# One fixed order of the four mixers for the shared preparation buffers in a decoder trunk

## The chip, the cores and the metric

The kernel runs on one core of a Trainium2 chip. The metric is the device time of one execution in microseconds (us), as the median of several runs. A NeuronCore has a matrix engine (TensorE, PE in the profile; its weight loads are the row PEld), a vector engine (VectorE, DVE), a scalar engine (ScalarE, ACT), a general engine (GpSimd, POOL) and a sync engine (SyncE, SP) that issues the DMA transfers here. Each engine works through its own queue strictly in order; they wait for one another by semaphores.

## What is computed

Two layers (DEPTH = 2) of a decoder trunk over 256 tokens of width 1024 in float32. Cut to what matters here:

```python
for l in range(DEPTH):
    h = rms_norm(x, norm1_g[l])
    proj = h @ w_in[l]                      # one projection, split among four mixers and the gates
    ya = dsa_mixer(...)                     # A, sparse: an indexer picks 64 keys per query
    yb = moba_mixer(...)                    # B, block attention
    yc = nsa_mixer(...)                     # C, compressed blocks (an MLP), selected blocks, window
    yd = swa_mixer(...)                     # D, sliding window of 128 with sinks
    br = einsum('bsnc,ncd->bsnd', stack(ya, yb, yc, yd), w_branch[l])
    x = x + (sigmoid(g_br) * br).sum(n) @ w_out[l]
    x = x + conv_ffn(rms_norm(x, norm2_g[l]), w_up[l], conv_w[l], conv_b[l], w_down[l])
```

Every mixer normalises its heads and applies rotary positions before it attends. In C, the raw keys and values are cut into 15 overlapping blocks, and a hidden layer (weights `c_cmp_w1`, then GELU, then `c_cmp_w2`) compresses each.

## The kernel before

**Weights.** All products are made to float32 accuracy from fp32r pieces. A weight chunk is loaded by DMA into one of three buffers `raw`; `split_hi` (ACT) rounds a piece of it to `hi`, `split_lo` (DVE) makes the rest, `lo = raw - hi`; there are four buffers of each. PE multiplies a piece as `hi` with `ahi`, `hi` with `alo` and `lo` with `ahi`, where `ahi` and `alo` are the two parts of the activations. A piece of 128x1024 is 12 matmuls of 512 columns. The stream of these pieces goes through the whole kernel; `SEQ` fixes in which order the merge gates, the hidden layer of C and the branch projections take their chunks: gate 0 (two halves), hidden 0 and 1, gate 1, branch 0, gate 2, branch 1, gate 3 (first half), branch 2, branch 3 (first half), and the last halves.

**Mixers.** Beside this stream run the mixers as generators: `dsa` (A), `moba` (B), `nsa` (C), `swa` (D). Each starts by taking the one set of preparation buffers in the ring `prep_r` (`rt`, `qr`, `kr`, `kn`), forms normalised and rotated queries and keys there on DVE, ACT and POOL (POOL computes the inverse roots `rD`, `rC` and so on by a power), transposes them on PE (`T_pairs`), gives the set back, and spawns its attention (`attend2`: scores, `softmax`, `values`). C prepares more: its rotated keys and copied values are transposed, copied to `kn`, and summed with the block encoding into `kr`, from which `hidden` on PE computes the compression layer with weights that stay in `raw` until it has run. When that sum exists, `hid.ready` is set; `main`, the one generator that emits the weight stream on PE, does not go on past `hidden` before.

**Order.** Nothing of this order is decided on the chip. `Flow.run` is a planner that runs while the kernel is built: again and again it takes, of all generators, the one whose next step can start first by its own clock model, and among equals the one of lower priority number (`PRIO` for the mixers, `urgent` for the pieces, 40 for `main`). The step is emitted at the end of its engine's queue, and there it stays. So the set of preparation buffers goes to whichever mixer's first step the planner sees first. In layer 0 that gave A, B, C, D; in layer 1 it gave A, B, D, C. In this kernel `swa` has priority number 6, in front of `nsa` with 7 and of `moba` with 19.

Where the text speaks of PSUM banks: the weight stream, the scores of the first token half and the hidden layer share the four banks `mm`; the scores of the second half use `sc`; transposes and values use `tr`. All instructions have the helper's line L214 in the profile, so places are found by tile names and by time.

Of the kernel before, what the change touches and what calls it, by code (L numbers as in the profile page):

```python
# [231 lines left out]
def trunk(ctx: ExitStack, tc: tile.TileContext, a, out):  # L232
# [15 lines left out]
    def ring(n, shape, name, dt=F32):  # L248
# [12 lines left out]
    prep_r = Ring([(sb([128, NT, 512], "rt"), sb([128, NT, 256], "qr"), sb([128, NT, 256], "kr"),  # L261
                    sb([128, NT, 256], "kn"))])
# [73 lines left out]
    col_f = [Fut() for _ in range(DEPTH)]  # L336
    tab_f = [Fut() for _ in range(DEPTH)]
# [61 lines left out]
           ("branch", 1, 0), ("branch", 1, 1), ("gate", 3, 0), ("branch", 2, 0), ("branch", 2, 1),  # L399
           ("branch", 3, 0), ("gate", 3, 1), ("branch", 3, 1)]  # L400
    FIRST, LAST = [n for op, n, _ in SEQ if op == "branch"][0], SEQ[-1][1]
    PRIO = (4, 19, 7, 6)
    PORDER = (0, 2, 1, 3)
    CH_A, CH_C = [(0, 384), (384, 680)], [(1448, 1832), (1832, 2100)]
    CH_B, CH_D = [(680, 1192), (1192, 1448)], [(2100, 2612)]
# [393 lines left out]

    def dsa(l, pa, pf, y, yf):  # L800
        m = M[l]
        (prep,) = yield "ACT", [pf, col_f[l]], [prep_r]
        rt, qr, kr, kn = prep
        latT = kn[:, :, 128:256]
        tl = yield from head_rstd(pa[:, :, None, 256:384], 1, 128, sm1["rl"], rt, [])
        tb, = yield "PE", [], [tr_r]
        tp = tb[:, :256].rearrange("p (t q) -> p t q", t=NT)
        for t in range(NT):
            te = P.transpose(tp[:, t, :], pa[:, t, 256:384], ident)
        yield "ACT", [te], []  # L810
        te = A.activation(latT, tp, AF.Copy, scale=m["col"][:, 16:17])
        tr_r.give(tb, te)
        tb, = yield "PE", [te], [tr_r]
        kvp = tb[:, :256].rearrange("p (t q) -> p t q", t=NT)
        for t in range(NT):
            te = P.matmul(kvp[:, t, :], latT[:, t, :], m["kvup"], start=True, stop=True)
        ti = yield from head_rstd(pa[:, :, None, 640:672], 1, 32, sm1["ri"], rt, [])
        yield "DVE", [te, tl], []
        tkv = V.tensor_tensor(kvA, kvp, sm1["rl"][:, :, None].to_broadcast([128, NT, 128]), op=ALU.mult)
        tr_r.give(tb, tkv)  # L820
        yield "DVE", [tab_f[l]], []
        tq = yield from rope(qr.rearrange("p t (h u d) -> p t h u d", u=1, d=32), heads(pa[:, :, 384:640], 32), 8, 32,
                             cosi, sini, rt, [])
        (ix,) = yield "PE", [], [qk_r]
        iqT, ikT = ix[:, 0:512].rearrange("p (k s) -> p k s", k=2), ix[:, 512:768].rearrange("p (k s) -> p k s", k=1)
        tq = yield from T_pairs(iqT, qr, 2, [tq])
        yield "DVE", [ti], []
        ikn = kn[:, :, None, 0:32]
        tn = V.tensor_tensor(ikn, pa[:, :, None, 640:672], sm1["ri"][:, :, None, None].to_broadcast([128, NT, 1, 32]), op=ALU.mult)
        krd = kr[:, :, 0:128]  # L830
        tk = yield from rope(krd.rearrange("p t (h u d) -> p t h u d", h=1, d=32), ikn, 1, 32, ci, si, rt, [tn], dup=4)
        tk = yield from T_pairs(ikT, krd, 1, [tk])
        iw = th(sm1["iw"], 8)
        yield "DVE", [], []
        V.tensor_scalar(iw, pa[:, :, 672:680], 1.0 / 16.0, None, op0=ALU.mult)
        idx_d = []
        idx_f = Fut()
        fin = qk_done(ix, idx_d, idx_f, NT)
        self_f = [Fut() for _ in range(NT)]
        for t in range(NT):  # L840
            fl.spawn(indexer(t, iqT, ikT, iw, [tq, tk], fin, self_f[t]), 5 + t)
        trk = yield from head_rstd(kvA[:, :, None, 0:64], 1, DH, sm1["rk"], rt, [tkv])
        yield "DVE", [trk], []
        knv = kn[:, :, None, 0:64]
        tn = V.tensor_tensor(knv, kvA[:, :, None, 0:64], sm1["rk"][:, :, None, None].to_broadcast([128, NT, 1, 64]), op=ALU.mult)
        tk = yield from rope(krd.rearrange("p t (h u d) -> p t h u d", h=1, d=64), knv, 1, DH, cc[:, 1], ss_[:, 1], rt, [tn], dup=2)
        trq = yield from head_rstd(heads(pa[:, :, 0:256]), H, DH, sm1["rqA"], rt, [])
        yield from scaled(sm1["sA"], sm1["rqA"], H, trq)
        tq = yield from rope(qr.rearrange("p t (h u d) -> p t h u d", u=1, d=64), heads(pa[:, :, 0:256]), H, DH,
                             cc[:, 0], ss_[:, 0], rt, [])  # L850
        (qk,) = yield "PE", [], [qk_r]
        qT, kT = qk[:, 0:512].rearrange("p (k s) -> p k s", k=2), qk[:, 512:768].rearrange("p (k s) -> p k s", k=1)
        tq = yield from T_pairs(qT, qr, 2, [tq])
        tk = yield from T_pairs(kT, krd, 1, [tk])
        prep_r.give(prep, tk)
        fin = qk_done(qk, [], yf, 1)
        fl.spawn(attend2(10, qT, lambda h: 0, kT, lambda h, b: kvA[:, b, 64:128], th(sm1["sA"], H), sel,
                        y, [tq, tk] + self_f, fin=fin), 10)
# [35 lines left out]
        f.t = V.tensor_tensor(sel[t], sel[t], mask, op=ALU.min)  # L894

    def moba(l, pb, pf, y, yf):
        (prep,) = yield "ACT", [pf, tab_f[l]], [prep_r]
        rt, qr, kr, kn = prep
        tr = yield from head_rstd(heads(pb[:, :, 0:512]), 8, DH, sm1["rB"], rt, [])
        yield from scaled(sm1["sB"], sm1["rB"], 8, tr)  # L900
        tq = yield from rope(qr.rearrange("p t (h u d) -> p t h u d", u=1, d=64), heads(pb[:, :, 0:256]), H, DH,
                             cc[:, 2], ss_[:, 2], rt, [])
        (qk,) = yield "PE", [], [qk_r]
        qT, kT = qk[:, 0:512].rearrange("p (k s) -> p k s", k=2), qk[:, 512:1024].rearrange("p (k s) -> p k s", k=2)
        tq = yield from T_pairs(qT, qr, 2, [tq])
        yield "DVE", [], []
        tn = V.tensor_tensor(heads(kn), heads(pb[:, :, 256:512]),
                        th(sm1["rB"], 8)[:, :, 4:8, None].to_broadcast([128, NT, H, DH]), op=ALU.mult)
        tk = yield from rope(kr.rearrange("p t (h u d) -> p t h u d", u=1, d=64), heads(kn), H, DH, cc[:, 3], ss_[:, 3], rt, [tn])
        tk = yield from T_pairs(kT, kr, 2, [tk])  # L910
        prep_r.give(prep, tk)
        fin = qk_done(qk, [], yf, 1)
        fl.spawn(attend2(20, qT, lambda h: h // 2, kT, lambda h, b: pb[:, b, 512 + 64 * h:576 + 64 * h],
                        th(sm1["sB"], H), [tri[:, 128:], tri], y, [tq, tk], fin=fin), 20)

    def swa(l, pd, pf, y, yf):
        (prep,) = yield "ACT", [pf, tab_f[l]], [prep_r]
        rt, qr, kr, kn = prep
        tr = yield from head_rstd(heads(pd[:, :, 0:384]), 6, DH, sm1["rD"], rt, [])
        yield from scaled(sm1["sD"], sm1["rD"], 6, tr)  # L920
        tq = yield from rope(qr.rearrange("p t (h u d) -> p t h u d", u=1, d=64), heads(pd[:, :, 0:256]), H, DH,
                             cc[:, 8], ss_[:, 8], rt, [])
        (qk,) = yield "PE", [], [qk_r]
        qT, kT = qk[:, 0:512].rearrange("p (k s) -> p k s", k=2), qk[:, 512:1024].rearrange("p (k s) -> p k s", k=2)
        tq = yield from T_pairs(qT, qr, 2, [tq])
        yield "DVE", [], []
        knv = heads(kn[:, :, 0:128])
        tn = V.tensor_tensor(knv, heads(pd[:, :, 256:384]),
                        th(sm1["rD"], 6)[:, :, 4:6, None].to_broadcast([128, NT, 2, DH]), op=ALU.mult)
        tk = yield from rope(kr.rearrange("p t (h u d) -> p t h u d", h=2, d=64), knv, 2, DH, cc[:, 9], ss_[:, 9], rt, [tn], dup=2)  # L930
        tk = yield from T_pairs(kT, kr, 2, [tk])
        prep_r.give(prep, tk)
        fin = qk_done(qk, [], yf, 1)
        fl.spawn(attend2(30, qT, lambda h: h // 2, kT,
                        lambda h, b: pd[:, b, 384 + 64 * (h // 2):448 + 64 * (h // 2)], th(sm1["sD"], H),
                        [tri[:, 128:], dmask], y, [tq, tk], sink=M[l]["sink"], fin=fin), 30)

    def nsa(l, pc, pf, y, yf, hid):
        m = M[l]
        (prep,) = yield "DVE", [pf, tab_f[l]], [prep_r]  # L940
        rt, qr, kr, kn = prep
        kvd = kr.rearrange("p t (i u d) -> p t i u d", i=2, u=2)
        t1 = yield from rope(kvd[:, :, 0:1], pc[:, :, None, 256:320], 1, DH, cosd, sind, rt, [], dup=2)
# [322 lines left out]
    def main():  # L1266
# [13 lines left out]
        for l in range(DEPTH):  # L1280
# [11 lines left out]
            proj = (pa, pb, pc, pd)  # L1292
            ys = [p[:, :, 0:256] for p in proj]
            yf = [Fut() for _ in range(4)]
            def mixer(n, f):
                if n == 2:
                    fl.spawn(nsa(l, pc, f, ys[2], yf[2], hid), PRIO[2])
                else:
                    fl.spawn((dsa, moba, None, swa)[n](l, proj[n], f, ys[n], yf[n]), PRIO[n])


            banks = []
            for i, kg in [(0, 0), (1, 0), (0, 1), (1, 1)] + [(i, kg) for i in range(2, len(COLS)) for kg in range(2)]:
                n, c0, c1 = COLS[i]
# [4 lines left out]
                if kg == 1:  # L1309
                    f = Fut()  # L1310
# [176 lines left out]
```

## Time and profile before

| what | before |
|---|---|
| median of 3 runs | 851.69 us (851.65 to 853.23) |
| the profiled execution's own time | 850.18 us |
| its span, first to last instruction | 848.4 us |
| PE matmul busy | 835.4 us, 98% |
| PE weight loads busy | 733.1 us, 86% |
| DVE busy | 673.0 us, 79% |
| ACT busy | 543.8 us, 64% |
| POOL busy | 36.5 us, 4% |
| granted TensorE clock, mean | 0.994 |
| DMA | 149.91 MB, 177 GB/s on average |

The busy shares are averages over stages: the projections, mixers and gates of layer 0 take the time to about 245 us, its feed-forward part that to about 425 us, and layer 1 repeats both. The span leaves out some 1.8 us of the execution's own time, before the first and behind the last instruction.

### The profile page before, as it was taken

To read this page: it belongs to the slowest core of one execution; us is meant where nothing else is said; L and a number is where in the kernel's file an instruction comes from. 1 tells how busy PE (TensorE), PEld (TensorE's weight loads), DVE (VectorE), ACT (ScalarE), POOL (GpSimd) and SP (SyncE) were. 2 spreads that over 40 slices of the span, in tenths; PEclk is the share of its full clock that TensorE was granted. 3 is DMA by queue.
4 is the path that set the end of the run, shared out by engine and by line. 5 is a ranking of instruction groups with operands and counts; after the bars stand their busy time and mean duration, and the time that the engine had idled before them with its cause. 6 is when DMAs were issued, how large, how long until landed. Compare 5 with 4: busy or idle time off the path is not lost.

```text
span 848.4 us, 14190 instructions
## 1 busy us (share of the span) xinstructions
PE 835.4 (98%) x5459; PEld 733.1 (86%) x5459; DVE 673.0 (79%) x1327; ACT 543.8 (64%) x941; POOL 36.5 (4%) x33
## 2 busy tenths in 40 slices
PE   9999999999999999999999997999999999999998
PEld 8987787888899999978898875878878999999886
DVE  5799989788579999975458989977676799999552
ACT  6673775765478888844366667766445788888431
POOL 0111111000000000000001110100000000000000
PEclk9999999999999999999999997999999999999999
DMA  7754563444647666546456453435455465665550
GB/s 264 248 199 149 178 216 106 159 162 153 219 138 229 207 201 197 186 153 210 132 168 211 157 173 115 148 117 182 162 192 192 149 199 199 200 199 199 175 197 26
DMA packets 103414, 149.91 MB, mean 177 GB/s; under 512 B 4072, under 2 KB 62258, under 8 KB 103346
## 3 DMA queue, kind: packets, MB, share of 16 engines
q1 hardware_dynamic: 103346, 149.00, 52.6%
q8 instruction: 43, 0.70, 0.3%
q14 instruction: 25, 0.20, 0.1%
HBM read 147.94 MB, written 1.05 MB: 176 GB/s over the span
## 4 chain that ended last, share of the span: by engine, by line
PE 86%; DVE 7%; DMA 2%; POOL 2%; ACT 1%; issue 1%; SPq 0%; DVEq 0%; ACTq 0%
PE mm L214 75%; PE tr L214 6%; PE sc L214 5%; DVE lo L214 2%; DMA raw<-in_w_in_dram 1%; POOL rB L214 1%; DVE acc L214 1%; DVE rt L214 1%; DMA x<-in_x_dram 1%; POOL rD L214 1%; DVE m L214 1%; DVE f L214 1%; ACT f L214 0%; ACT hi L214 0%; SPq L242 0%
## 5 line engine op out<-in xcount | busy, mean ns | idle before, releaser
L214 DVE TENSOR_TENSOR lo<-raw,hi 128x1024 fp32r<-128x1024 f32 (+2 forms) x280 | 328.7, 1179 | 99.4 <-ACT hi L214 95.3
L214 ACT ACTIVATE hi<-raw 128x1024 fp32r<-128x1024 f32 (+2 forms) x280 | 283.0, 1022 | 152.6 <-PE mm L214 132.4
L214 PE MATMUL mm<-hi,ahi 128*128 128x512 f32 (+4 forms) x480 | 176.0, 372 | 0.6 <-ACT hi L214 0.6
L214 PE MATMUL mm<-hi,alo 128*128 128x512 f32 (+4 forms) x480 | 172.2, 364 | 0.0
L214 PE MATMUL mm<-ahi,hi 128*128 128x256 f32 x640 | 149.9, 276 | 0.0
L214 PE MATMUL mm<-alo,hi 128*128 128x256 f32 x640 | 149.7, 276 | 0.0
L214 PEld LDWEIGHTS mm<-alo,hi 128*128 128x128 f32 x640 | 120.1, 188 | 0.1
L214 PEld LDWEIGHTS mm<-ahi,hi 128*128 128x128 f32 x640 | 120.2, 188 | 0.1
L214 PE MATMUL mm<-lo,ahi 128*128 128x512 f32 (+4 forms) x480 | 118.2, 369 | 0.0
L214 PEld LDWEIGHTS mm<-hi,ahi 128*128 128x128 f32 x480 | 90.2, 188 | 15.2 <-issue 1.7
L214 PEld LDWEIGHTS mm<-hi,alo 128*128 128x128 f32 x480 | 90.3, 188 | 12.0
L214 PEld LDWEIGHTS mm<-lo,ahi 128*128 128x128 f32 x480 | 83.0, 188 | 13.2 <-issue 1.3
L214 PE MATMUL mm<-hi,slotQ 128*128 128x512 f32 x352 | 89.6, 395 | 0.0
L214 PE MATMUL mm<-ahi,lo 128*128 128x256 f32 x640 | 86.9, 276 | 0.0
L214 PEld LDWEIGHTS mm<-hi,slotQ 128*128 128x128 f32 x352 | 66.1, 188 | 15.4
L214 PEld LDWEIGHTS mm<-ahi,lo 128*128 128x128 f32 x640 | 79.1, 188 | 0.0
L214 ACT ACTIVATE f<-f,col 128x256 f32<-128x256 f32 x88 | 48.1, 594 | 6.4 <-DVE f L214 6.4
L214 PE MATMUL mm<-lo,slotQ 128*128 128x512 f32 x176 | 48.7, 396 | 0.0
L214 PEld LDWEIGHTS mm<-lo,slotQ 128*128 128x128 f32 x176 | 33.0, 188 | 7.6
L214 ACT ACTIVATE qk<-f,col 128x256 f32<-128x256 f32 x88 | 39.2, 495 | 0.0
L214 ACT ACTIVATE f<-f,nmx 128x128 f32<-128x128 f32 (+1 forms) x80 | 35.3, 444 | 4.7 <-DVE nmx L214 4.7
L214 DVE SCALAR_TENSOR_TENSOR f<-f,col,f 128x254 f32<-128x254 f32 x88 | 38.2, 478 | 0.0
(235 smaller groups left out, 1038.6 us busy)
## 6 DMA issues: line engine op xcount, KB each, us to landing
raw<-in_w_up_dram SPq DMA_DIRECT2D x44, 1024.0 KB, 5.0
raw<-in_w_in_dram SPq DMA_DIRECT2D x40, 1024.0 KB, 4.8
raw<-in_w_down_dram SPq DMA_DIRECT2D x20, 1024.0 KB, 4.9
raw<-in_w_out_dram SPq DMA_DIRECT2D x8, 1024.0 KB, 5.3
raw<-in_w_branch_dram SPq DMA_DIRECT2D x6, 1024.0 KB
raw<-in_w_in_dram SPq DMA_DIRECT2D x7, 768.0 KB
raw<-in_w_in_dram SPq DMA_DIRECT2D x4, 592.0 KB, 3.7
raw<-in_w_in_dram SPq DMA_DIRECT2D x4, 536.0 KB, 5.7
```

Of the source, the lines that this page charges most:

```text
L214: fn(*a, **k)
```

## The change

The set of preparation buffers now goes round in a written order. Each mixer gets, beside the future of its projection, a turn: A's is open from the start, and a mixer that has taken the set opens the next one's turn (`next_turn`). The order is A, B, C, D (sparse, block, compressed, sliding) in both layers. `nsa` names ACT and no longer DVE as the engine of its empty first step, which only the planner sees. And the priority number of `swa` goes from 6 to 21, behind `moba`.

```diff
--- before.py
+++ after.py
@@ -399,7 +399,7 @@
            ("branch", 1, 0), ("branch", 1, 1), ("gate", 3, 0), ("branch", 2, 0), ("branch", 2, 1),
            ("branch", 3, 0), ("gate", 3, 1), ("branch", 3, 1)]
     FIRST, LAST = [n for op, n, _ in SEQ if op == "branch"][0], SEQ[-1][1]
-    PRIO = (4, 19, 7, 6)
+    PRIO = (4, 19, 7, 21)
     PORDER = (0, 2, 1, 3)
     CH_A, CH_C = [(0, 384), (384, 680)], [(1448, 1832), (1832, 2100)]
     CH_B, CH_D = [(680, 1192), (1192, 1448)], [(2100, 2612)]
@@ -799,7 +799,8 @@
 
     def dsa(l, pa, pf, y, yf):
         m = M[l]
-        (prep,) = yield "ACT", [pf, col_f[l]], [prep_r]
+        (prep,) = yield "ACT", [pf[0], pf[1], col_f[l]], [prep_r]
+        pf[2]()
         rt, qr, kr, kn = prep
         latT = kn[:, :, 128:256]
         tl = yield from head_rstd(pa[:, :, None, 256:384], 1, 128, sm1["rl"], rt, [])
@@ -894,7 +895,8 @@
         f.t = V.tensor_tensor(sel[t], sel[t], mask, op=ALU.min)
 
     def moba(l, pb, pf, y, yf):
-        (prep,) = yield "ACT", [pf, tab_f[l]], [prep_r]
+        (prep,) = yield "ACT", [pf[0], pf[1], tab_f[l]], [prep_r]
+        pf[2]()
         rt, qr, kr, kn = prep
         tr = yield from head_rstd(heads(pb[:, :, 0:512]), 8, DH, sm1["rB"], rt, [])
         yield from scaled(sm1["sB"], sm1["rB"], 8, tr)
@@ -914,7 +916,8 @@
                         th(sm1["sB"], H), [tri[:, 128:], tri], y, [tq, tk], fin=fin), 20)
 
     def swa(l, pd, pf, y, yf):
-        (prep,) = yield "ACT", [pf, tab_f[l]], [prep_r]
+        (prep,) = yield "ACT", [pf[0], pf[1], tab_f[l]], [prep_r]
+        pf[2]()
         rt, qr, kr, kn = prep
         tr = yield from head_rstd(heads(pd[:, :, 0:384]), 6, DH, sm1["rD"], rt, [])
         yield from scaled(sm1["sD"], sm1["rD"], 6, tr)
@@ -937,7 +940,8 @@
 
     def nsa(l, pc, pf, y, yf, hid):
         m = M[l]
-        (prep,) = yield "DVE", [pf, tab_f[l]], [prep_r]
+        (prep,) = yield "ACT", [pf[0], pf[1], tab_f[l]], [prep_r]
+        pf[2]()
         rt, qr, kr, kn = prep
         kvd = kr.rearrange("p t (i u d) -> p t i u d", i=2, u=2)
         t1 = yield from rope(kvd[:, :, 0:1], pc[:, :, None, 256:320], 1, DH, cosd, sind, rt, [], dup=2)
@@ -1292,7 +1296,17 @@
             proj = (pa, pb, pc, pd)
             ys = [p[:, :, 0:256] for p in proj]
             yf = [Fut() for _ in range(4)]
+            order_of = ((0, 1, 2, 3), (0, 1, 2, 3))[l]
+            turn = dict((n, Fut()) for n in order_of)
+            turn[order_of[0]].t = 0.0
+
+            def next_turn(n):
+                i = order_of.index(n) + 1
+                if i < 4:
+                    turn[order_of[i]].t = 0.0
+
             def mixer(n, f):
+                f = [f, turn[n], lambda: next_turn(n)]
                 if n == 2:
                     fl.spawn(nsa(l, pc, f, ys[2], yf[2], hid), PRIO[2])
                 else:
```

The sum of the instructions stays; the planner emits them in another order. The order of the DMA loads on SP is the same as before, row for row. On DVE three copies out of PSUM go to another engine.

The first place is DVE in layer 1, from the last `lo` piece in front of the moved work. Before (`rD`, `sD`: the inverse root and the scale of the sliding mixer; `f_1`: softmax rows of the sparse mixer):

```order
L214 TENSOR_TENSOR lo_79<-raw_72,hi_75 128x1024
L214 TENSOR_REDUCE rD<-rt 128x12
L214 RECIPROCAL rd_113<-den_111 128x4
L214 TENSOR_SCALAR rD<-rD 128x12
L214 TENSOR_SCALAR f_1_83<-f_1_83,rd_113 128x256 x2
L214 TENSOR_SCALAR sD<-rD 128x8
L214 TENSOR_TENSOR rt<-slotQ,cc 128x2x256
L214 TENSOR_TENSOR rt<-slotQ,ss 128x2x256
L214 TENSOR_TENSOR qr<-rt 128x8x32 x2
```

Now, from the same piece (`kn<-tr` and `kr<-kn,col`: the input of C's hidden layer; `rC`, `sC`: the compressed mixer's inverse root and scale):

```order
L214 TENSOR_TENSOR lo_79<-raw_72,hi_75 128x1024
L214 TENSOR_TENSOR rt<-slotQ,cst 128x2x64 x2
L214 RECIPROCAL rd_113<-den_111 128x4
L214 TENSOR_TENSOR kr<-rt 128x2x2x32 x2
L214 TENSOR_SCALAR f_1_83<-f_1_83,rd_113 128x256 x2
L214 COPY kn<-tr_69 64x512
L214 COPY kn<-tr_69 64x2x255
L214 TENSOR_TENSOR kr<-kn,col_143 128x8x15 x4
L214 TENSOR_REDUCE rC<-rt 128x8
L214 TENSOR_SCALAR rC<-rC 128x8
L214 TENSOR_TENSOR lo_80<-raw_72,hi_76 128x1024
L214 TENSOR_SCALAR sC<-rC 128x8
```

The sliding mixer's preparation is gone from here, and the compressed mixer's stands in its place. Behind `sC` come one more `lo` piece, `ylo` of the sparse mixer, and then the reads of the block mixer's scores out of `mm_65` and `mm_66`.

The second place is PE in layer 1, around the hidden layer (`mm_65<-raw_73,kr`: hidden 0, the first product with the weights in `raw`). Before:

```order
L214 MATMUL tr_69<-cst,qr 128x128 x4
L214 MATMUL mm_63<-lo_79,ahi 128x512
L214 MATMUL mm_64<-lo_79,ahi 128x512
...
L214 MATMUL tr_70<-cst,kr 128x128 x4
L214 MATMUL tr_69<-cst,kr 128x128 x4
L214 MATMUL tr_70<-cst,f_0_82 128x128 x4
L214 MATMUL mm_65<-raw_73,kr 15x128 x16
L214 MATMUL mm_66<-raw_71,kr 15x128 x16
```

Now:

```order
L214 MATMUL tr_70<-cst,f_1_83 128x128 x4
L214 MATMUL tr_69<-cst,kr 128x128 x4
L214 MATMUL mm_63<-lo_78,ahi 128x512
L214 MATMUL mm_64<-lo_78,ahi 128x512
...
L214 MATMUL mm_63<-lo_79,ahi 128x512
L214 MATMUL mm_64<-lo_79,ahi 128x512
...
L214 MATMUL mm_65<-raw_73,kr 15x128 x16
L214 MATMUL mm_63<-raw_71,kr 15x128 x16
```

Before, two transposes of `kr` (the sliding mixer's, then the compressed mixer's) and one of softmax rows stood between the last piece of gate 0 and the hidden layer. Now the compressed mixer's transpose of `kr` stands sixteen matmuls of the weight stream, the sparse mixer's values and the block mixer's scores earlier, and the hidden layer follows directly on the last piece of gate 0. The bank of hidden 0 is `mm_65` as before, that of hidden 1 is `mm_63`, which gate 0 has just filled.

In layer 0 the order of buffers was A, B, C, D already; there the sliding mixer's preparation and attention move behind the compressed mixer's last attention on PE, DVE, ACT and POOL, because of its new priority number.

## Rows read from the trace of the kernel before

**Rows 1.** Page, part 1: busy us (share of the span) xinstructions.

```profile
PE 835.4 (98%) x5459; PEld 733.1 (86%) x5459; DVE 673.0 (79%) x1327; ACT 543.8 (64%) x941; POOL 36.5 (4%) x33
```

**Rows 2.** Windows of 5 us around the hidden layer in layer 1.

```profile
core 0: us, PE busy (x) PEld busy (x) DVE busy (x) ACT busy (x) POOL busy (x), PEclk, DMA share, GB/s
510.00:515.00 5.00, 5.00 (x52) 3.93 (x48) 4.96 (x16) 3.81 (x5) 0.00 (x0) 1.00 0.02 5
515.00:520.00 5.00, 1.31 (x5) 0.72 (x4) 4.54 (x19) 2.48 (x9) 0.00 (x0) 0.72 0.61 211
520.00:525.00 5.00, 2.88 (x28) 2.34 (x32) 4.39 (x16) 4.91 (x18) 0.00 (x0) 0.50 0.00 0
```

**Rows 3.** Windows: same stretch of both layers, the slow clock, 40 us of layer 1.

```profile
51.80:251.60 199.80, 199.04 (x1204) 163.93 (x1204) 167.74 (x418) 124.92 (x245) 13.44 (x8) 1.00 0.48 163
462.90:674.20 211.30, 205.07 (x1216) 168.45 (x1216) 169.80 (x422) 126.78 (x243) 10.95 (x8) 0.98 0.48 161
517.40:527.80 10.40, 6.77 (x78) 5.07 (x79) 9.13 (x36) 8.61 (x26) 1.64 (x1) 0.52 0.24 84
515.00:555.00 40.00, 34.19 (x261) 26.93 (x261) 36.25 (x130) 28.16 (x72) 3.85 (x3) 0.87 0.45 158
```

**Rows 4.** Timeline, PE, layer 1: start us, us, instruction [idle before <-releaser].

```profile
513.69 0.60 PE L214 MATMUL tr<-cst,qr 128*128 128x128 f32 x4
514.05 1.18 PE L214 MATMUL mm<-lo,ahi 128*128 128x512 f32 x4
518.21 1.09 PE L214 MATMUL tr<-cst,kr 128*128 128x128 f32 x4 [2.98 <-DVE kr L214]
521.10 1.09 PE L214 MATMUL tr<-cst,kr 128*128 128x128 f32 x4 [1.80 <-DVE den L214]
...
524.06 3.55 PE L214 MATMUL mm<-raw,kr 128*15 128x128 f32 x64 [1.02 <-DVE kr L214]
...
528.39 0.48 PE L214 MATMUL mm<-hi,ahi 128*128 128x512 f32 x1
```

**Rows 5.** Timeline, DVE, layer 1.

```profile
504.39 1.23 DVE L214 TENSOR_TENSOR lo<-raw,hi 128x1024 fp32r<-128x1024 f32 x1
505.53 0.95 DVE L214 TENSOR_REDUCE rD<-rt 128x12 f32<-128x768 f32 x1
...
519.33 0.69 DVE L214 COPY qk<-tr 128x512 f32<-128x512 f32 x1 [0.46 <-PE tr L214]
...
522.22 1.39 DVE L214 COPY kn<-tr 64x512 f32<-64x512 f32 x2 [0.46 <-PE tr L214]
523.65 1.16 DVE L214 TENSOR_TENSOR kr<-kn,col 128x120 f32<-128x120 f32 x4
```

**Rows 6.** Timeline, ACT, layer 1.

```profile
510.57 2.00 ACT L214 ACTIVATE hi<-raw 128x1024 fp32r<-128x1024 f32 x2 [1.07 <-DMA raw<-in_w_in_dram]
512.78 0.59 ACT L214 COPY slotQ<-tr 128x512 f32<-128x512 f32 x1 [0.20 <-PE tr L214]
513.40 0.63 ACT L214 ACTIVATE yhi<-slotQ 128x512 fp32r<-128x512 f32 x1
```

**Rows 7.** Timeline, POOL, layer 1.

```profile
525.68 1.64 POOL L214 TENSOR_TENSOR rC<-rC,mhalf 128x8 f32<-128x8 f32 x1 [16.61 <-DVE rd L214]
```

**Rows 8.** Timeline, PE: the hidden layer in layer 0.

```profile
101.92 1.94 PE L214 MATMUL mm<-raw,kr 128*15 128x128 f32 x64
```

**Rows 9.** Timeline, PE and DVE, layer 1: a `lo` piece where it is used soonest.

```profile
570.74 1.07 PE L214 MATMUL mm<-lo,ahi 128*128 128x512 f32 x4
573.49 1.08 PE L214 MATMUL mm<-lo,ahi 128*128 128x512 f32 x4
...
569.02 1.22 DVE L214 TENSOR_TENSOR lo<-raw,hi 128x1024 fp32r<-128x1024 f32 x1
```

## The prediction, made before the change was run

> **What bounds the kernel now.** I read the page's busy shares first, then windows over the span, then the chain of waits and the timelines of single engines where the windows show a hole. The page says that PE is busy 98% of the span [rows 1], so what can be gained is PE's idle time, and what is lost while its clock is low. Almost all of that lies in one place: in layer 1, between 515 and 525 us, PE is busy 1.31 and 2.88 us of 5, while just ahead it was busy all the time [rows 2]. The granted clock, 1.00 ahead of it, is 0.50 in the second of these windows, which is the lower level, 1.2 GHz instead of 2.4.
>
> The timeline of PE shows who waits there. After the last `lo` matmuls of gate 0, PE waits 2.98 us to transpose the `kr` of the sliding mixer, 1.80 us to transpose the `kr` of the compressed mixer, and 1.02 us for the input of the hidden layer; the weight stream goes on at 528.39 us [rows 4]. All three end on DVE's work (the middle one is put down to a small softmax step that stands just ahead of the `kr` it needs). On DVE the reader sees why: the sliding mixer's preparation, from the sum for `rD` at 505.53 to the copy of its keys at 519.33, runs first, and the compressed mixer's copies to `kn` and sums to `kr`, for which `hidden` stands in PE's queue, come only at 522.22 and 523.65 [rows 5]. PE's queue is in order: the whole weight stream stands behind `hidden`.
>
> Layer 0 is the control in the same trace, since its buffers go A, B, C, D already. From the second half of the indexer to the first matmul of the feed-forward part that uses a bank `sc`, layer 0 takes 199.80 us and PE idles 0.76 of them, at clock 1.00; layer 1 takes 211.30 and idles 6.23 [rows 3]. Layer 1's stretch holds 12 matmuls more, one weight piece, which is 2.75 us by the spacing of two neighbours [rows 9]. So the order of layer 1 costs 11.50 - 2.75 = 8.75 us against layer 0.
>
> **What the change does to it.** (1) *The stall goes.* Idle time is 3.69 + 2.12 = 5.81 us in the two windows [rows 2]. The clock is low from about 517.4 to 527.8, and in that time PE is busy 6.77 us [rows 3]; at the full clock half of that would do, so 3.4 us are lost: 9.2 us together. The hidden layer alone shows the factor: 3.55 us here [rows 4], 1.94 in layer 0 [rows 8]. That 9.2 agrees with the 8.75 plus layer 0's own 0.76 is a check on the sum.
>
> (2) *What wait is left.* Follow DVE in the new order, from the end of its last unchanged `lo` at 505.6 [rows 5]. Rotation of the compressed keys and two softmax rows, some 1.6 us of short instructions, end at 507.2; PE then transposes `kr` (0.36 us by the step from the transpose to what follows it [rows 4], and the same again of handoffs) until 508. The two copies to `kn` and the four sums to `kr`, 1.3 and 1.1 us without overlap [rows 5], end at 510.5, and the sum for `rC` at 511.2. So the input of `hidden` is there 13 us sooner than now, and is no longer what `hidden` waits for. That is now its bank: `mm_65` is freed when DVE has read two of the block mixer's scores, and in DVE's queue these stand behind `lo`, `sC`, `lo`, `ylo`. The first of these `lo` needs a `hi` that ACT makes from 510.57 because it waits for a load [rows 6]; nothing in the change moves that load. So `lo` runs from 511.6 to 512.8, `sC` waits for POOL's `rC`, 1.64 us here [rows 7], until about 513.2, the second `lo` ends at 514.4, `ylo` at 515.0, two score reads at 515.6; with a handoff `hidden` starts at about 515.9. PE has its stream done at 515.2 as now (one transpose of four goes from ahead of that point, another takes its place). The wait is 0.7 us. Below, it may be nothing, if the load lands sooner; above, the nearest row is the whole present wait, 5.8 us and the low clock with it. I take 0.7, since all the parts are rows of this very place.
>
> (3) *Work that only moves.* Before, four transposes of queries, four of keys and twelve of softmax rows had been done by 528.39; they now come later, at full clock. In (1) they are counted at full clock already, so this adds nothing. Check: `hidden` from 515.9, plus 1.94, plus some 1.9 for these, makes 519.7 against 528.39, so 8.7 us sooner, against 9.2 - 0.7 = 8.5.
>
> (4) *What the sliding mixer costs later.* Its 15 preparing instructions on DVE, about 5.3 us without overlap from the first to the last [rows 5], and one power on POOL, now stand behind the compressed mixer's last preparation. DVE is busy 36.25 us of the 40 from 515 to 555 [rows 3], so there is little room, and PE arrives 8.5 us sooner. What covers it: every `lo` piece ahead of the moved work gains from its absence. By counting the rows ahead of each `lo` in both orders with the durations of the trace (an estimate), DVE has 5 to 15 us less to do ahead of each piece in that region, and 14 us less ahead of the one with the smallest lead, ended at 570.2 and used at 573.49 [rows 9]. If that cover were gone, PE would wait for `lo` by up to 8.5 less the lead, about 5 us. I take 0.4 us for new small waits in this layer: layer 0, with the same order, shows 0.76 in the stretch, and layer 1 has 6.23 - 5.81 = 0.42 outside the stall already [rows 3]. Bounds 0 and 5.
>
> (5) *Layer 0.* Only the sliding mixer moves back there. Its last product now stands where the compressed mixer's stood, and the softmax of the compressed mixer's two attentions comes closer behind their scores: about 34 matmuls of 0.23 us between the first of these scores and their transposes, 7.8 us, where a softmax with its queue takes some 5 to 8. I take 0.5 us of new waits; bounds 0 and 3, the upper one the longest PE wait of the trace [rows 4].
>
> (6) *At nothing:* the loads keep their order on SP, and raw buffers of the hidden weights are given back sooner; the empty first step of `nsa` issues nothing; three copies move from DVE to ACT, which idles a third of the time [rows 1]. The feed-forward parts keep their orders.
>
> Sum: -9.2 + 0.7 + 0.4 + 0.5 = -7.6 us. Against the profiled execution's own 850.18 us (848.4 of span) that gives 842.6; the median of the runs shown is 1.5 above that execution, so **844.1 us** for the median.
>
> **The rivals.** *VectorE becomes the bound.* For it: 91% busy in those 40 us [rows 3]. If the sooner start of PE is only passed on as far as DVE can close its own idle time, 3.75 us in that window, the kernel gains 3.75 and ends at about 847.9. Against it: the sliding mixer's work leaves the front of DVE's queue. The Trainium skill, "Perfetto Trace Analysis", Identifying the Most-Contended Engine, says that matmul occupancy is no good measure, and to judge TensorE by its weight loads and the others by occupancy. By that rule VectorE at 36.25 of 40 us would stand ahead of the weight loads at 26.93 [rows 3], and this rival would be the forecast. The trace agrees only in part: in that window PE idles nowhere but in the stall, and layer 0 runs the same work at 0.76 us of idle time.
>
> *The wait stays in another dress.* `hidden` waits for `mm_65` behind three in-order waits of DVE (transpose, POOL, ACT). If that is late by about 4 us, the clock falls again, as it did during the 2.98 us wait [rows 4], and the gain is 9.2 - 4 - 3.4 = 1.8 at most: about 850 to 852, no change. Against it: each part above is a row.
>
> *Slower: the sliding mixer comes too late in both layers.* It is now last in both, and branch 3 waits for its `ylo`. In layer 1, 28 matmuls of the stream, 6.4 us, lie between its values and branch 3; what must fit in are a copy out of PSUM, `yhi` and `ylo`, some 2 us with handoffs [rows 6]. If its values themselves wait, PE stands still with nothing else in its queue. A stall as dear as the present one, 9.2 us, in both layers gives 850.18 - 7.6 + 18.4, and 1.5 for the median: 862.5. It is slower than before from about 4.7 us of new stall in each layer on. Against it: layer 0's sliding mixer has more cover than that.
>
> **How the numbers follow.** A measurement of this kernel tells differences above about 0.2%, 1.7 us. Forecast (841.8 to 846.5): 0.65. No wait left and none new (842 or a little below): 0.03. VectorE the bound (846.5 to 849.9): 0.15. Other dress, no change: 0.09. Slower: 0.08. So faster 0.83, same 0.09, slower 0.08. The range from 841.8 to 849.9 takes in the forecast and the first rival, some 0.8; its ends are the bounds of (2), (4) and (5) taken one at a time.
>
> **What would show it.** Right: PE's transpose of `kr` ahead of the last piece of gate 0; `hidden` in layer 1 takes about 1.94 us at clock 1.00; PE idles under 2 us between 510 and 530; the feed-forward part of layer 1 starts about 8 us sooner. Wrong: a PE wait of 3 us or more anywhere, with the granted clock at half after it; look ahead of `hidden` (released by DVE's score reads), at `lo` pieces released by DVE, and ahead of branch 3 (released by `ylo`).

## The result, and the profile after

The changed kernel takes 842.62 us in the median (842.49 to 842.81, 4 runs), the kernel before, measured beside it, 851.67 (849.28 to 853.23, 4 runs): a ratio of 0.9896, 95% interval 0.9873 to 0.992. It is faster by over 0.2%. The forecast was 844.1, in a range from 841.8 to 849.9. The profiled execution takes 842.65 us, 7.53 less than that of before (850.18); the sum of the prediction was 7.6.

The page of the changed kernel, part 1, against [rows 1]:

```profile
PE 834.4 (99%) x5459; PEld 733.1 (87%) x5459; DVE 672.6 (80%) x1324; ACT 543.6 (65%) x944; POOL 35.5 (4%) x33
```

No engine has appreciably less to do; the span became shorter by idle time and by the clock. The windows around the hidden layer of layer 1, against [rows 2], and the same stretch of both layers, from the second half of the indexer to the first feed-forward product in a bank `sc`, against [rows 3]:

```profile
core 0: us, PE busy (x) PEld busy (x) DVE busy (x) ACT busy (x) POOL busy (x), PEclk, DMA share, GB/s
515.00:520.00 5.00, 4.53 (x78) 3.40 (x76) 4.91 (x21) 1.26 (x2) 0.00 (x0) 1.00 0.67 233
520.00:525.00 5.00, 5.00 (x24) 4.15 (x25) 3.94 (x12) 4.70 (x15) 0.00 (x0) 1.00 1.05 388
...
515.00:555.00 40.00, 39.47 (x271) 31.17 (x270) 35.76 (x108) 24.57 (x51) 4.45 (x3) 1.00 0.59 205
...
52.08:252.78 200.70, 199.80 (x1204) 163.89 (x1204) 166.26 (x417) 125.55 (x246) 12.97 (x8) 1.00 0.47 162
464.06:666.68 202.62, 201.91 (x1217) 166.54 (x1216) 170.49 (x421) 125.79 (x245) 10.89 (x8) 1.00 0.49 168
```

The clock stays at 1.00. Layer 1's stretch fell from 211.30 to 202.62 us, 8.68 less: 5.52 of it idle time of PE (6.23 to 0.71), 3.16 busy time of PE for the same work, which ran in part at the lower clock before. Layer 0's grew by 0.90. The part behind is the same (174.2 us), and the indexer of layer 0 starts 0.28 later (43.60 to 43.88). Together -8.68 + 0.90 + 0.28 = -7.50, the whole difference of the spans (848.4 to 840.9). PE's timeline around the hidden layer, against [rows 4]:

```profile
508.48 0.60 PE L214 MATMUL tr<-cst,kr 128*128 128x128 f32 x4
...
515.31 1.07 PE L214 MATMUL mm<-lo,ahi 128*128 128x512 f32 x4
516.86 1.94 PE L214 MATMUL mm<-raw,kr 128*15 128x128 f32 x64 [0.47 <-DVE mx L214]
518.73 0.50 PE L214 MATMUL mm<-hi,ahi 128*128 128x512 f32 x1
```

DVE around it, against [rows 5]:

```profile
509.12 1.39 DVE L214 COPY kn<-tr 64x512 f32<-64x512 f32 x2 [0.87 <-PE tr L214]
510.54 1.17 DVE L214 TENSOR_TENSOR kr<-kn,col 128x120 f32<-128x120 f32 x4
511.63 0.67 DVE L214 TENSOR_REDUCE rC<-rt 128x8 f32<-128x512 f32 x1
...
512.76 1.23 DVE L214 TENSOR_TENSOR lo<-raw,hi 128x1024 fp32r<-128x1024 f32 x1 [0.25 <-ACT hi L214]
514.26 0.17 DVE L214 TENSOR_SCALAR sC<-rC 128x8 f32<-128x8 f32 x1 [0.27 <-POOL rC L214]
514.34 1.22 DVE L214 TENSOR_TENSOR lo<-raw,hi 128x1024 fp32r<-128x1024 f32 x1
515.47 0.69 DVE L214 TENSOR_TENSOR ylo<-slotQ,yhi 128x512 fp32r<-128x512 f32 x1
516.17 0.35 DVE L214 CUSTOM_DVE_ANT_0 f<-mm,cst,sB 128x128 f32<-128x128 f32 x1
516.45 0.08 DVE L214 DVE_READ_ACCUMULATOR2_ANT mx<- 128x1 f32 x1
```

The transpose of `kr` stands at 508.48, ahead of the last piece of gate 0, and the sum that `hidden` needs ends at 511.7. `hidden` starts only at 516.86, released by `mx`: DVE's reads of the block mixer's scores, which free the bank. That is the wait that the prediction put at 0.7 us; it is 0.47. The three waits of DVE that stand ahead of those reads are there too, for PE's transpose (0.87), for ACT's `hi` (0.25) and for POOL's `rC` (0.27), as named. Layer 1 starts 1.18 us later in this execution (453.89 us for 452.71, by the indexer's first product). With that taken off, the sum for `hidden` ends at 510.5 and `hidden` starts at 515.7, where the prediction had 510.5 and 515.9.

### The profile page after: what moved, and what is told of

Read it like the earlier page. It is cut to its first block, busy times and chain, and to the rows that moved or that the text cites. A ratio compares the mean times of both kernels' runs of the same rounds, so it can differ in the third digit from the quotient of the medians.

```text
span 840.9 us, 14190 instructions
## 1 busy us (share of the span) xinstructions
PE 834.4 (99%) x5459; PEld 733.1 (87%) x5459; DVE 672.6 (80%) x1324; ACT 543.6 (65%) x944; POOL 35.5 (4%) x33
## 4 chain that ended last, share of the span: by engine, by line
PE 87%; DVE 7%; ACT 2%; POOL 1%; issue 1%; DVEq 0%; ACTq 0%
PE mm L214 76%; PE tr L214 6%; PE sc L214 5%; DVE lo L214 2%; ACT f L214 1%; DVE acc L214 1%; DVE f L214 1%; POOL rB L214 1%; DVE m L214 1%; ACT hi L214 1%; DVE rt L214 1%; POOL rD L214 0%; DVE mg L214 0%; DVE rB L214 0%; DVE slotP L214 0%
## 5 line engine op out<-in xcount | busy, mean ns | idle before, releaser
L214 PEld LDWEIGHTS mm<-hi,alo 128*128 128x128 f32 x480 | 90.9, 189 | 12.1
```

Source lines behind the costliest of these rows:

```text
L214: fn(*a, **k)
```

## The experiments

In what follows, stretch 0 and stretch 1 run from the first product of the indexer (`sc<-qk`) of a layer to the feed-forward part; PE's busy time in them is from windows at just these times. The 221.50 us in the expectations is this length for layer 1 of the kernel before, from 452.71 to 674.21; the words "second half of the indexer" in them are a slip, that half starts 10.2 us later, and the differences agree within 0.03. Each ratio is to the kernel before as it was measured beside that run (medians 851.16, 851.27 and 850.83 us; 851.67 for the changed kernel). Tile names that are new: `slotP` holds a gated branch product, `hsum` the row sums of the hidden layer, `kcd` the compressed keys, `Pc` the softmax weights of the compressed blocks. All times in us.

| kernel | median | ratio to before, 95% | stretch 0 | stretch 1 | PE idle in stretch 1 |
|---|---|---|---|---|---|
| before | 851.7 | 1 | 208.00 | 221.50 | 6.23 |
| changed | 842.62 | 0.9873 to 0.992 | 208.90 | 212.79 | 0.71 |
| 1 turns only | 844.01 | 0.9905 to 0.9932 | 207.97 | 214.85 | 2.39 |
| 2 priority only | 855.96 | 1.0042 to 1.007 | 208.99 | 225.59 | 7.77 |
| 3 late in layer 1 only | 842.19 | 0.9883 to 0.991 | 208.13 | 212.78 | 0.72 |
| 4 before, 60 products in the wait | 854.55 | 1.0034 to 1.0059 | 208.05 | 225.92 | 0.51 |
| 5 before, 20 products in the wait | 849.99 | 0.9977 to 0.9995 | 207.87 | 221.34 | 4.08 |
| 6 changed, three `lo` twice | 845.13 | 0.9915 to 0.994 | 208.83 | 215.64 | 2.18 |
| 7 changed, ten `lo` twice | 853.53 | 1.0015 to 1.0035 | 209.41 | 223.17 | 8.80 |
| 8 compressed ahead of block | 859.9 | 1.0085 to 1.0119 | 208.21 | 232.90 | 11.95 |
| 9 before, 24 products, order kept | 849.76 | 0.9977 to 0.9995 | 207.95 | 221.08 | 2.63 |
| 10 changed, three `lo` twice in the feed-forward part | 843.35 | 0.9889 to 0.9919 | 208.80 | 213.55 | 1.25 |
| 11 before, again | 851.12 | 0.9995 to 1.0016 | 207.87 | 222.80 | 6.65 |

The stretches are those of one profiled execution each. Run 10 and the changed kernel have the same program up to the end of stretch 1 and differ there by 0.8 us, the two profiles of before by 1.3; smaller differences of stretch 1 between two kernels are not told apart.

**1 and 2: which of the two edits does it.** The changed kernel with the old priority number, and the kernel before with the new one and no turns:

```diff
-    PRIO = (4, 19, 7, 21)
+    PRIO = (4, 19, 7, 6)
```

> The changed kernel with the sliding mixer's priority number back at 6; the written turns stay, so in layer 1 the compressed mixer still gets the buffers ahead of the sliding one. Theory (the order of the buffers in layer 1 alone removes the stall of 5.8 us idle and the 3.4 us of low clock): hidden 0 of layer 1 takes about 1.94 us at a granted clock of 1.00, and the median is 841.5 to 844. Rival (the priority number does it): the stall ahead of hidden is back, hidden takes over 3 us, 849 to 853.

```diff
-    PRIO = (4, 19, 7, 6)
+    PRIO = (4, 19, 7, 21)
```

> The kernel before with the sliding mixer's priority number 21 and no turns. In layer 1 the sliding mixer still gets the buffers ahead of the compressed one. Theory (order of the buffers): the stall stays, PE waits some 5 to 6 us between 510 and 530 us, hidden 0 takes about 3.5 us at half the clock, and layer 0 loses the 0.9 us that the changed kernel loses there: 849 to 854. Rival (the priority number does it): 842 to 844.

The turns alone take stretch 1 to 214.85, 6.65 below before; the stall ahead of `hidden` is gone there, and the median, 844.01, lies at the upper end of what was expected. (The engine that the first step of `nsa` names goes with the turns in this run; the two are not told apart.) The priority alone makes it 4.09 longer, and its median, 855.96, lies 2 us above the range expected. Its waits on PE, in order of time:

```profile
518.68 0.66 PE L214 MATMUL tr<-cst,qr 128*128 128x128 f32 x4 [2.24 <-DVE qr L214]
521.46 1.11 PE L214 MATMUL tr<-cst,f 128*128 128x128 f32 x4 [2.13 <-ACT f L214]
524.47 1.97 PE L214 MATMUL tr<-cst,f 128*128 128x128 f32 x8 [1.05 <-DVE f L214]
...
532.29 1.94 PE L214 MATMUL mm<-raw,kr 128*15 128x128 f32 x64 [0.22 <-DVE kr L214]
535.99 0.40 PE L214 MATMUL tr<-cst,hsum 128*128 128x15 f32 x2 [1.76 <-DVE hsum L214]
```

The sliding mixer still holds the preparation buffers ahead of the compressed one, so everything that `hidden` needs stands behind it; with the low priority it only holds them longer, and `hidden` starts 6.5 us later from the layer's start (77.89 us after it; 71.35 before). One detail was expected wrongly: `hidden` itself takes 1.94 us there, at full clock, since the low clock (0.56 and 0.50 from 520 to 530 us) has passed by then; PE then waits 1.76 us for its row sums. On top of the turns the same number helps by 2.06 us in stretch 1. Without it DVE works on the sliding mixer's scores between reads of the branch products, and PE waits for those banks:

```profile
595.18 0.51 PE L214 MATMUL mm<-hi,ahi 128*128 128x512 f32 x1 [0.54 <-DVE slotP L214]
...
596.71 0.50 PE L214 MATMUL mm<-hi,ahi 128*128 128x512 f32 x1 [0.79 <-DVE slotP L214]
```

So the two edits are not additive: -6.65 and +4.09 alone, -8.71 together.

**3: layer 0.** The priority number 21 in layer 1 only.

```diff
-    PRIO = (4, 19, 7, 21)
+    PRIO = ((4, 19, 7, 6), (4, 19, 7, 21))
...
-                    fl.spawn((dsa, moba, None, swa)[n](l, proj[n], f, ys[n], yf[n]), PRIO[n])
+                    fl.spawn((dsa, moba, None, swa)[n](l, proj[n], f, ys[n], yf[n]), PRIO[l][n])
```

> The changed kernel with priority number 21 for the sliding mixer in layer 1 only; layer 0 has 6 again. Theory (layer 0's stretch lost 0.9 us, 199.8 to 200.7, because the sliding mixer moved back there): 0.9 us less than the changed kernel, about 841.7. Rival (that 0.9 us is scatter or comes from elsewhere): within 0.3 us of the changed kernel, 842.3 to 842.9.

Stretch 0 is 208.13, 0.77 shorter than in the changed kernel, and stretch 1 the same to 0.01 us. Runs 1 and 2 say the same of layer 0 (207.97 without the number, 208.99 with it). In the medians the 0.43 us stay within the scatter, so this is the best version by its stages, but not one that the times can tell from the changed kernel.

**4, 5 and 9: what does the low clock cost by itself?** The prediction counted 5.8 us of idle time and 3.4 us of low clock. Here PE is kept busy in the kernel before while it waits, with products that are overwritten by the hidden layer, so that the clock stays up and the wait remains. In runs 4 and 5 `hidden` issues them for as long as the planner's own clock says that its input is not there. In run 9 their number is written down (`spare` issues them, which is L1050 in the profile, two rows each; 12 in front of the sliding mixer's transposes, 8 in `nsa`, 4 here). Its edit in `hidden`:

```diff
-        ps, = yield "PE", [hid.ready, ch.loaded], [mm_r]
+        ps, = yield "PE", [], [mm_r]
+        first = l == 1 and i == 0
+        if first:
+            fill[:] = [ps]
+            spare(12)
+        yield "PE", [hid.ready, ch.loaded], []
+        if first:
+            spare(4)
```

> The kernel before, with about 60 products of 128x128 put into PE's queue where PE waits for hidden 0's input in layer 1; their results are overwritten by the hidden layer. They fill the wait without shortening it. Theory (the stall costs 5.8 us of idle time plus 3.4 us of low clock, and the clock falls because PE idles): the granted clock stays 1.00 over 515 to 530, hidden 0 takes about 1.94 us, and the time is 2.5 to 3.5 us below the kernel before, about 848.5. Rival (the low clock costs nothing that counts, since DVE sets the pace there, or the clock falls all the same): within 1 us of the kernel before, 850.7 to 852.7.

> As the filled kernel before it, but with 20 added products, not 60: one of them took 0.223 us of PE there (0.67 us for three), so that 60 were 13.4 us where the wait is 5.8; 9, 6, 1 and 4 of them now stand in the waits, 4.5 us in all. Theory (5.8 us of idle time and 3.4 us of low clock are separate losses): the clock stays at 1.00 or falls later, hidden 0 takes about 1.94 us, layer 1's stretch from the second half of the indexer to the feed-forward part is 3 to 3.5 us shorter than the 221.50 of the kernel before, some 218.2, and the median is about 848. Rival (DVE sets the pace behind the stall, so the clock costs nothing, or the clock falls all the same): the stretch stays at 221 to 222, the median at 850.5 to 852.

> The kernel before with 24 added products of 0.223 us in the three waits (12, 8, 4), and every other instruction in its old place on every engine, so that no new order blurs the answer: in the run with 20 products the row sums of the hidden layer moved ahead of the weight stream and PE waited 0.94 us for them. Theory of the prediction (the low clock's 3.4 us are a loss of their own): layer 1's stretch 218.1 instead of 221.50, 847.9 in the median. Second theory (DVE sets the pace up to the hidden layer's input, so the clock only costs there and behind: 3.55 - 1.94 = 1.6 us on the hidden layer, up to 0.8 on the transposes beside it): 219.1 to 220.0, 849 to 850. Third (the clock costs nothing): 221.5, 851.

Run 4 missed its aim: its products took 0.223 us each, 13.4 us in all, and pushed `hidden` back by 5.9 us, to 530.23 (77.22 after the layer's start, 71.35 before). Run 5 was blurred by a new wait of 0.94 us. In run 9 the products of PE stand in the same order as before, but for the added ones. Its timeline of PE:

```profile
514.78 2.84 PE L1050 MATMUL mm<-cst 128*128 128x128 f32 x24
518.42 0.63 PE L214 MATMUL tr<-cst,kr 128*128 128x128 f32 x4 [0.80 <-DVE kr L214]
518.89 1.95 PE L1050 MATMUL mm<-cst 128*128 128x128 f32 x16
...
523.88 1.94 PE L214 MATMUL mm<-raw,kr 128*15 128x128 f32 x64 [0.49 <-DVE kr L214]
```

And its windows, to be held against [rows 2]:

```profile
515.00:520.00 5.00, 4.20 (x38) 4.04 (x37) 5.00 (x20) 2.02 (x7) 0.00 (x0) 1.00 0.61 211
520.00:525.00 5.00, 4.18 (x67) 3.52 (x68) 4.37 (x14) 5.00 (x19) 0.00 (x0) 1.00 0.01 3
```

The clock stays at 1.00, and `hidden` takes 1.94 us, not 3.55. Yet it starts 71.44 us after the layer's start (71.35 before), because DVE's chain to its input sets that. Of the 1.6 us that it saves, 1.3 are left where the weight stream goes on (526.81 us, 74.37 after the layer's start; 75.68 before). Behind that PE waits 0.44 us for `hsum` from DVE, which it didn't before. At the end of stretch 1, 221.08, the gain is 0.42 against the first profile of before and 1.72 against the second (run 11); the median is 1.1 us lower (849.76 against 850.83, a ratio of 0.9986). So the first theory falls, and the third falls by the medians, since the interval of their ratio leaves out 1. The second has its median (849 to 850) but not its stretch (219.1 to 220.0). The low clock's 3.4 us are real time of PE, but while DVE sets the pace, PE gives most of it back as idle time.

**6, 7 and 10: is VectorE the bound by now?** In the changed kernel DVE makes some `lo` pieces twice, with the same values: three (6) or ten (7) of those between 515 and 555 us, and three others in the feed-forward part (10). The edit of run 6; 7 and 10 differ in the numbers of the pieces:

```diff
+                if issued[0] in (177, 180, 183):
+                    nc.vector.tensor_tensor(pc.lo, v, pc.hi.bitcast(F32), op=ALU.subtract)
                 pc.lo_f.t = V.tensor_tensor(pc.lo, v, pc.hi.bitcast(F32), op=ALU.subtract)
```

> The changed kernel in which DVE makes three of the lo pieces between 515 and 555 us of layer 1 twice (the second writes the same values): 3 x 1.2 = 3.6 us more of DVE work, where DVE is busy 35.76 of 40 us and idle 4.24. Theory (PE is the bound and DVE works ahead of it): the time stays within 0.3 us of the changed kernel, layer 1's stretch stays at 212.8. Rival (VectorE is the bound by now): each us of DVE costs a us, 846 or so, stretch 216.4.

> The same with ten lo pieces made twice, 12.1 us more of DVE work in these 40 us, nearly three times DVE's idle time there. Theory (DVE works some us ahead of PE, and what it falls behind it can catch up later): some of it shows, 2 to 8 us, in waits of PE for lo, since 12.1 - 4.2 = 7.9 us don't fit into the window. Rival (VectorE is the bound by now): all 12 us show, about 854.5, stretch 224.9.

> The changed kernel with three lo pieces made twice in the feed-forward part of layer 1 (about 706, 733 and 755 us), 3.6 us more of DVE work, where DVE is busy 38.32 and 37.37 of 40 us, more than the 35.76 of 40 from 515 to 555 us, and PE all the time. Theory (three doubled pieces cost 2.9 us of layer 1's stretch because DVE and PE wait for one another there in the mixers' chains; in the feed-forward part DVE only feeds a stream, with a lead): within 0.5 us of the changed kernel, the part behind the stretch stays at 174.2 to 174.7. Rival (the busy share decides): 2.9 us or more, 845.5 or above, the last part 177.

The theory that DVE works ahead of PE fell: 3.6 us more of DVE work lengthen stretch 1 by 2.85 us, 2.1 against run 10, which has the changed kernel's program up to there; 12.1 us lengthen it by 10.4 (9.6 against run 10). The rival, that every us shows, came near but not whole. PE's waits in run 7:

```profile
529.82 1.27 PE L214 MATMUL tr<-cst,f 128*128 128x128 f32 x4 [1.55 <-DVE f L214]
...
545.74 0.23 PE L214 MATMUL tr<-cst,kcd 15*128 15x15 f32 x1 [1.23 <-DVE kcd L214]
550.67 0.41 PE L214 MATMUL tr<-cst,kr 128*128 128x128 f32 x2 [0.84 <-DVE kr L214]
...
558.43 0.41 PE L214 MATMUL tr<-cst,Pc 128*128 128x128 f32 x2 [1.87 <-DVE Pc L214]
```

None is for `lo`. PE waits for the mixers' own steps, which stand behind the doubled pieces in DVE's queue and are needed by transposes. Run 10 is the control, by windows in its feed-forward part:

```profile
690.00:730.00 40.00, 40.00 (x356) 40.00 (x355) 38.48 (x53) 32.23 (x52) 0.00 (x0) 1.00 0.62 206
730.00:770.00 40.00, 40.00 (x356) 40.00 (x355) 38.81 (x54) 32.39 (x53) 0.00 (x0) 1.00 0.56 187
```

DVE is busier there, 38.5 of 40 us, and three pieces of the same size cost nothing: PE is busy all the time, and the part behind stretch 1 takes 174.2 us, as in the changed kernel. The 0.73 us by which the median of run 10 is higher, more than the 0.5 expected, lie ahead of that part: in its profile stretch 1 is 0.76 longer and the indexer of layer 0 starts 0.64 later. DVE's busy share alone doesn't tell the two places apart.

**8: the compressed mixer further ahead.** Run 3 with another order in layer 1:

```diff
-            order_of = ((0, 1, 2, 3), (0, 1, 2, 3))[l]
+            order_of = ((0, 1, 2, 3), (0, 2, 1, 3))[l]
```

> The changed kernel with priority number 21 for the sliding mixer in layer 1 only, and with the order sparse, compressed, block, sliding in layer 1, so that the hidden layer's input is prepared earlier still and its bank doesn't wait for the block mixer's scores. Theory (what is left there is the 0.5 us wait for that bank): layer 1's stretch 0.5 us shorter than 212.8, median about 841.7. Rival (the block mixer, now behind, is late somewhere else): a new wait of a us or more, 843 or above.

The wait in front of `hidden` is gone, it starts at 514.25 us. But DVE reads the block mixer's scores only at 586.6 us (516.2 in the changed kernel), with the branches close behind, and PE stands still for the softmax rows:

```profile
580.70 0.66 PE L214 MATMUL tr<-cst,f 128*128 128x128 f32 x4 [1.48 <-ACT f L214]
583.48 1.97 PE L214 MATMUL tr<-cst,f 128*128 128x128 f32 x8 [2.12 <-DVE f L214]
594.58 0.95 PE L214 MATMUL tr<-cst,f 128*128 128x128 f32 x4 [3.91 <-DVE f L214]
```

Stretch 1 is 20.1 us longer than in the changed kernel, of it 11.2 idle time and 8.9 busy time, the latter at a clock of 0.83 from 575 to 595 us and 0.66 from 595 to 610. The rival was right, and by far more than it said: this is a case like the prediction's slower one (a mixer too late for the branches, no other work in PE's queue), but in layer 1 alone and with the block mixer late.

**11: why before scatters.**

> The kernel before, unchanged, for another profile of it: are the 1.5 us between the profiled execution (850.18) and the median (851.7) in the first loads or in the stall? If in the loads, the indexer's second half starts later than the 43.60 us of the first profile and the stretches keep 208.0 and 221.5; if in the stall, layer 1's stretch differs from 221.5 by a us or more.

It is both. This execution, 853.66 us, has the indexer's first product at 45.90 us (43.60 before), and stretch 1 of 222.80. Of the 1.30 us of stretch 1, 0.42 are idle time of PE (its first wait is 3.34 us for 2.98) and 0.88 busy time. The low clock comes later: it lasts from 521.7 to 531.9 us, for 517.4 to 527.6 in the first profile, which is 2.1 us later from the layer's start, and so reaches further past the stall:

```profile
520.72 0.63 PE L214 MATMUL tr<-cst,kr 128*128 128x128 f32 x4 [3.34 <-DVE kr L214]
523.16 1.41 PE L214 MATMUL tr<-cst,kr 128*128 128x128 f32 x4 [1.80 <-DVE den L214]
...
526.44 3.61 PE L214 MATMUL mm<-raw,kr 128*15 128x128 f32 x64 [1.02 <-DVE kr L214]
529.99 1.97 PE L214 MATMUL tr<-cst,f 128*128 128x128 f32 x8
...
530.00:535.00 5.00, 5.00 (x40) 4.37 (x38) 3.66 (x8) 1.19 (x3) 0.00 (x0) 0.81 1.03 378
```

The eight transposes behind `hidden` take 1.97 us here. In the first profile of before they took 1.09:

```profile
527.54 1.09 PE L214 MATMUL tr<-cst,f 128*128 128x128 f32 x8
```

## Why the prediction was right, step by step

(1) *The stall* was 9.2 us, and with the wait that is left (2) and the new small waits in layer 1 (4) the sum for this layer was -8.1. Stretch 1 fell by 8.7. By account the split holds as well: 5.5 us of idle time and 3.2 of busy time at the lower clock, where 5.81 - 0.7 - 0.4 = 4.7 and 3.4 stood. As causes the two are not separate. Run 9 shows that the clock alone is worth 0.4 to 1.7 us by the stretches, 1.1 by the medians, since most of what PE saves is waited for; the rest comes only together with the earlier input. And the order of layer 1 is not all of it: turns alone give 6.65, and 2.06 come from the priority number, which the prediction did not price apart.

(2) *The wait for the bank* was named rightly, with its releaser and all that stands in DVE's queue ahead of it; 0.47 us for 0.7.

(3) *Moved work at nothing:* the weight stream goes on behind `hidden` at 518.73 us, where 519.7 stood. That is 10.8 us sooner counted from the layer's start (64.84 after it, for 75.68); 8.7 us are left at the end of the stretch, and the 2.1 between are, by difference, the moved transposes, which now stand later (1.9 in the prediction).

(4) *New small waits in layer 1*, 0.4 us, did not come. PE's whole idle time in stretch 1 is 0.71, of which 0.47 is that bank; of the 0.24 left, 0.05 stands behind `hidden`. Outside the stall it was 0.42 before, so this term is -0.2: the 0.42 that it was taken from were in the kernel before already, and were no reason to add anything. The upper bound, 5 us, was not needed. The reason given, that `lo` gains a lead, was beside the point: runs 6 and 7 show that PE would have waited at the mixers' transposes, not at `lo`.

(5) *Layer 0*, 0.5 us of new waits, is 0.90 in all. Runs 1 to 3 put it on the sliding mixer's priority there. But little of it is waiting: PE's idle time in stretch 0 grows only from 0.76 to 0.90, while its busy time grows by 0.76 (207.24 to 208.00) with the same number of products (1252) at clock 1.00. Why they take longer in the new order is not shown. One new wait shows: at 199.45 us branch 3's last bank waits for DVE's read, where before there was none.

```profile
199.45 0.50 PE L214 MATMUL sc<-hi,yhi 128*128 128x512 f32 x1 [0.23 <-DVE slotP L214]
```

In layer 1 of the kernel before the same wait stood at 621.00 us, and it is gone there.

(6) *The 1.5 us from the profiled execution to the median* were added in vain for the changed kernel: its four runs lie within 0.32 us. Run 11 shows where they come from in the kernel before: up to 2.3 us from the start, which variants of the changed kernel have too (their indexer starts between 43.8 and 45.6 us; its own four runs don't show it), and 1.3 from the length of the waits and the place of the low clock in the stall, which went with the stall. The forecast's 844.1 is therefore 1.5 too high. The sum itself, 842.6, was met, but to 0.1 us only by luck: layer 1 gained 0.6 more than the sum for it, layer 0 lost 0.4 more, and the start came 0.28 later.

*The rivals.* VectorE as the bound (847.9) did not come, but what the prediction held against it, that PE idles nowhere else, was no evidence of slack: DVE has little between 515 and 555 us, where 2.1 to 2.85 of 3.6 added us are paid (run 6). The gain came whole because the change takes DVE work out from in front of `hidden`, and behind `hidden` PE still waits for next to nothing (0.05 us). The Trainium skill, "Perfetto Trace Analysis", Identifying the Most-Contended Engine, judges TensorE by its weight loads, beside its rate of arithmetic, and VectorE by its occupancy. By that rule VectorE leads in the changed kernel from 515 to 555 us (35.76 against 31.17 us), where added DVE work costs, and TensorE leads in run 10's feed-forward part (40.00 against 38.48 and 38.81), where it doesn't; these traces agree with it at both places, though the 847.9 that stood beside it did not come. The wait in another dress is the 0.47 us of (2), not 4. The slower case did not come either, since PE waits no more than 0.05 us behind `hidden` in layer 1 and 0.23 ahead of branch 3's last bank in layer 0. Run 8 shows that a case like it lies one swap of the order away.

## What to carry to other kernels

When engines share one set of buffers and the queues are in order, ask who holds the set while the longest stream waits, and let that consumer's producer have it first; then look at who becomes last. Idle time and low-clock time may be added up as an account of a stall, but the second is not a saving of its own: keep up the clock of the waiting engine alone, and most of the time comes back as waiting for the engine that sets the pace (1.1 of 3.4 us were left in run 9). A busy share says little on slack: double a few instructions in place and see what the stage pays.

## What the runs showed of the hardware

PE's granted clock stayed at 1.00 where the same waits were filled with products whose results nobody reads, and fell to 0.50 where they were not [rows 2]; it fell too in runs 2 and 8 behind their waits of 2 to 4 us. The Trainium skill, "TensorE: Matmul & The Clock Gate", Part 1 on the clock gate, says that the low clock is the default and that activity releases it; these runs agree with that direction. How far the low clock reaches past the same waits differs between executions of one program (to 527.6 and 531.9 us, and the 1.09 and 1.97 us above). The first 15 us also differ by 2 us: in run 11 PE waits 1.17 us for a load, and its first products follow one another at 0.32 us, where the same ones took 0.17 in the first profile of before (7.72 to 7.89 us). That is nearly the ratio of the two levels of the clock, but the granted clock in this window reads 1.00, so that it was the clock is not shown.

```profile
6.85 0.27 PE L214 MATMUL sc<-cst,rn 8*128 8x8 f32 x1 [1.17 <-DMA rn<-in_norm_g_dram]
...
10.15 0.52 PE L214 MATMUL mm<-hi,ahi 128*128 128x384 f32 x1
10.47 0.52 PE L214 MATMUL mm<-hi,alo 128*128 128x384 f32 x1
...
10.00:15.00 5.00, 5.00 (x25) 4.87 (x24) 3.04 (x6) 2.45 (x7) 0.00 (x0) 1.00 0.81 294
```
